# A hybrid layer on Trainium2: u projected by channel and laid out through DRAM, with the forget gates' columns moved into q's first chunk

## The chip, the cores and the metric

The kernel runs on one core of one Trainium2 chip. The metric is the device time of one execution in microseconds (us), the median of several runs. The engines of a core, as the profile names them, are PE (TensorE; PEld is its load of stationary operands), DVE (VectorE), ACT (ScalarE), POOL (GpSimd) and SP (SyncE, which here only issues DMAs).

## What is computed (the reference, cut to what matters)

One layer of a transformer: 1024 tokens of 1024 channels, a mixer of three kinds of heads, then a mixture of 16 experts. All of it is in fp32.

```python
proj = h @ w_in                      # h: 1024 x 1024, w_in: 1024 x 2568
u, q, k, v, f_logit, hc, bg, cg = split(proj, sizes 256, 512, 512, 512, 8, 256, 256, 256)
y_ssm  = s5_mixer(u, ...)            # 16 groups of 16 channels, 64 complex states each: a scan over tokens
y_attn = fox_attention(q, k, v, f_logit + forget_b, ...)   # cum = cumsum(log_sigmoid(f_logit)) biases the logits
y_conv = bg * short_conv(cg * hc)
x = x + gate1 * (rms_norm(concat(y_ssm, y_attn, y_conv)) @ w_out)
...
```

## The kernel before, in words

**Projections.** The normalised input stands transposed in SBUF, channels on the partitions, as two parts hTh and hTl, a rounded high part and the rest. The columns of w_in come in chunks of 256 (hc, cg, bg, u, and two halves each of q, k, v). SP loads each chunk's raw weights in four pieces (`wr`), ACT rounds each piece to its high part `wh` (L262) and POOL forms the low part `wl` (`feed`, L235). A product is then a group of 24 matmuls in `mm3` or `mm3_steps` (L272 to L283): eight of high by high (L275) and eight of low by high (L277), alternating, then eight of high by low (L280), which end the group. With conv's chunks the weights are stationary and 512 tokens move. With q, k and v a 128-token block of hT is stationary and 256 columns of weights move, so there are eight groups for each half of q and 16 for q.

**u.** In the kernel before u is made like q (`uf_group`, L948): eight groups, one for each j in 0 to 7, whose stationary operand is the 128 tokens j, j+8, j+16, ... of hT, a slice with a stride of eight elements, and whose 264 moving columns are u's 256 and the eight of f_logit. ACT writes the group's result into `u_tok` (L953), DVE copies the eight gate columns to `f_sb` (L954). `s5_main` (L769) then turns `u_tok` with 16 PE transposes (L776) and four ACT copies (L777) into `ug`, where a partition is (token within a block of eight, channel of a group) and a column is (group, block of eight).

**The scan.** From `ug` PE makes the blocks' inputs `px` (L790, four sets), DVE multiplies each by powers of the eigenvalue (six operations of `cmul`), runs two scans over 128 blocks (L799, L801), turns the result back (`t`, `vv`), and PE makes the outputs `py` (L826 to L829, four sets), ACT's gelu follows (L831), PE transposes the result for the GLU (L847), multiplies by its weights (`pgl`, L856), and `yd` goes to DRAM (L875).

**The order** is written by hand. Each engine works through its own instructions in the order in which the program issues them. The scan, the conv norm, the forget gates and the second ada product are generators, advanced by `step` (L958) at given places: `side` holds `s5_prep` (which makes the scan's tables; `pg` L684, L686) and then `s5_main`, `side2` holds `conv_norm` (ACT's squares `zt` L913, PE's `pn` L921 and `pb` L938) and later `ada2` (32 loads `adw` of 512 KB on SP, `pr` L1095), `side3` holds `f_chain` (L730). `smalls` (L268) puts a step between two matmuls of a group. US (L62) is the number of matmuls between such steps in u; PY (L57) the number of steps between the scan and `py`. In the loop over q and k (L1115) each group's result `pm` is evicted by ACT (`r`, L1133, and four squares `sq`, L1136); `qk_norm` (L1035) norms four groups at a time (13 small DVE operations `rk_...`, a product on DVE, one on POOL), splits them (`ks`), and `qk_turn` (L1058) transposes them (`ptk` L1061), copies to `qe` (L1067 on DVE, L1069 on ACT) and writes to DRAM from POOL (`qtd`, L1071). In this stage PSUM holds two buffers for `pm`, three for transposes, and three for `px`, `py`, `pgl` and `pr` together.

**f_chain** takes the log of the gates and sums it over tokens. Before, a partition holds a block of eight tokens: a DVE scan inside the block, a matmul with the strict triangle `triS` for the blocks ahead, and `cumd` is written from POOL in elements of 32 bytes for each partition and head.

## Time and profile before

| | |
|---|---|
| median of the runs | 1122.28 us (1121.11, 1122.28, 1126.86) |
| the profiled execution | 1124.22 us, of which the span in the profile is 1122.4 us |
| PE busy | 1026.0 us, 91% of the span |
| DVE, ACT, POOL busy | 722.0, 526.0, 311.7 us |
| stages | conv chunks until 122 us, u to 196, q to 277, k to 373, then v, attention, w_out and the experts |

The profiled execution is 1.94 us above the median, and its time is 1.82 us longer than the span. In the rows below, times are in us from the span's start. A line in the list of instructions gives the start, the duration, the engine, the source line, the operation, what is written and read, the shapes, and how many like it follow at once; in brackets stands the idle time before it and what ended that. A line of a stretch gives its begin, end and length, then the busy time of PE, PEld, DVE, ACT and POOL (with the number of instructions), the granted clock, the DMA engines' mean share and GB/s. A line of loads by form gives the count, the sum and the mean in ns of one. Matmul durations overlap: one matmul starts before the one before it has ended, so what a matmul costs is the distance of the starts. The granted clock (PEclk) is in shares of TensorE's full 2.4 GHz: 0.50 is its lower level, 1.2 GHz.

### The profile page before, as it was taken

The page shows a single profiled execution, that of the slowest core. Times are in us where ns is not written, and L with a number is a line of the kernel's source. Part 1 is how long each engine was busy: PE and PEld are TensorE (multiplying, and loading weights), DVE is VectorE, ACT ScalarE, POOL GpSimd, SP SyncE. Part 2 cuts the span into 40 slices and gives each one's busy share as a digit, 9 for nine tenths or more (in the row PEclk, how much of TensorE's full clock was granted, in tenths as well). Part 3 has the DMA queues.
Part 4 walks back from the last instruction along what each step waited for, and adds up shares of the span by engine and source line. Part 5 has one row for each costly group of instructions (what it writes and reads, how often), then busy time and mean ns, then how long its engine had stood idle before and what let it go on. Part 6 is the DMA issues. An engine that isn't in the chain of part 4 may idle for free. (4 is left out here: it accounts for less than half of the span.)

```text
span 1122.4 us, 18163 instructions
## 1 busy us (share of the span) xinstructions
PE 1026.0 (91%) x6383; PEld 849.1 (76%) x6383; DVE 722.0 (64%) x1564; ACT 526.0 (47%) x1107; POOL 311.7 (28%) x313
## 2 busy tenths in 40 slices
PE   0999899989999999899799994999999999999994
PEld 0578699978887988887688884677777777777773
DVE  2669702583345344687567778796667899789692
ACT  2351111444554555677532321764444676467470
POOL 4215930243321100138222233121422212122130
PEclk9999879989999999899889996799999999999998
DMA  9901103123787343557165733897788799979772
GB/s 190 355 22 39 38 10 78 39 67 110 224 273 255 102 126 105 159 155 230 35 194 188 243 133 107 301 339 244 233 269 281 238 366 357 375 240 353 253 242 41
DMA packets 102366, 213.53 MB, mean 190 GB/s; under 512 B 13998, under 2 KB 37020, under 8 KB 102108
## 3 DMA queue, kind: packets, MB, share of 16 engines
q1 hardware_dynamic: 89744, 170.93, 45.7%
q0 software_dynamic: 11680, 39.55, 13.0%
q10 hardware_dynamic: 828, 1.62, 0.4%
q8 instruction: 62, 1.02, 0.4%
q14 instruction: 52, 0.43, 0.1%
HBM read 184.41 MB, written 27.05 MB: 188 GB/s over the span
## 5 line engine op out<-in xcount | busy, mean ns | idle before, releaser
L94 DVE TENSOR_TENSOR wel<-wer,weh 128x1024 fp32r<-128x1024 f32 x192 | 223.4, 1219 | 2.2 <-ACT weh L1922 1.5
L1922 ACT ACTIVATE weh<-wer 128x1024 fp32r<-128x1024 f32 x192 | 188.9, 1053 | 4.8 <-DVE oh L1931 1.4
L1977 POOL DMA_INDIRECT out_dram<-y,idx x28 | 58.4, 2087 | 227.6 <-DVE y L2042 137.5
L2005 PE MATMUL pg<-weh,xh 128*128 128x512 f32 x256 | 104.7, 409 | 2.0 <-ACT hid L2163 0.7
L2006 PE MATMUL pg<-weh,xl 128*128 128x512 f32 x256 | 103.1, 403 | 0.0
L94 DVE TENSOR_TENSOR pl<-ptp,ph 128x512 fp32r<-128x512 f32 (+1 forms) x80 | 50.3, 636 | 39.5 <-ACT ph L1314 39.2
L2010 PE MATMUL pg<-wel,xh 128*128 128x512 f32 x256 | 66.5, 398 | 0.0
L2005 PEld LDWEIGHTS pg<-weh,xh 128*128 128x128 f32 x256 | 49.1, 192 | 17.9 <-issue 6.1
L1314 ACT ACTIVATE ph<-ptp 128x512 fp32r<-128x512 f32 (+1 forms) x80 | 44.2, 553 | 30.0 <-PE ptp L1309 29.2
L2006 PEld LDWEIGHTS pg<-weh,xl 128*128 128x128 f32 x256 | 49.1, 192 | 11.6 <-DVE xl L94 0.4
L2010 PEld LDWEIGHTS pg<-wel,xh 128*128 128x128 f32 x256 | 47.9, 189 | 11.3
L1296 ACT ACTIVATE lg<-lg,mn 128x128 f32<-128x128 f32 (+3 forms) x64 | 49.5, 774 | 10.6 <-DVE mn L1285 10.5
L1309 PE MATMUL ptp<-identF,lg 128*128 128x128 f32 x288 | 47.9, 285 | 6.2 <-DVE pl L94 6.0
L2032 PE MATMUL pd<-weh,hh 128*128 128x512 f32 x128 | 52.3, 408 | 0.7 <-ACT hh L2024 0.5
L275 PE MATMUL pmw<-woh,yh 128*128 128x512 f32 x128 | 52.7, 411 | 0.0
L277 PE MATMUL pmw<-woh,yl 128*128 128x512 f32 x128 | 51.2, 400 | 0.0
L2033 PE MATMUL pd<-wel,hh 128*128 128x512 f32 x128 | 50.6, 395 | 0.0
L1991 ACT ACTIVATE xh<-ptx 128x512 fp32r<-128x512 f32 x32 | 19.2, 599 | 62.2 <-issue 58.8
L1329 PE MATMUL po<-ph,vs 128*128 128x256 f32 (+1 forms) x160 | 47.1, 316 | 1.2 <-ACT ot L1333 1.0
L1961 POOL DMA_INDIRECT xg<-h2d,idx x16 | 20.7, 1294 | 89.5 <-DVE wgt L1948 62.5
L1330 PE MATMUL po<-pl,vs 128*128 128x256 f32 (+1 forms) x160 | 40.3, 286 | 0.2
L1133 ACT ACTIVATE r<-pm 128x256 f32<-128x256 f32 x32 | 12.3, 384 | 59.7 <-PE pm L280 55.6
(655 smaller groups left out, 2766.2 us busy)
## 6 DMA issues: line engine op xcount, KB each, us to landing
wer<-in_w_up_dram SPq DMA_DIRECT2D x64, 512.0 KB
wer<-in_w_gate_dram SPq DMA_DIRECT2D x63, 512.0 KB
wer<-in_w_down_dram SPq DMA_DIRECT2D x63, 512.0 KB
adw<-in_ada_w_dram SPq DMA_DIRECT2D x32, 512.0 KB
xt<-in_x_dram SPq DMA_DIRECT2D x16, 512.0 KB
vroom<-in_ada_w_dram SPq DMA_DIRECT2D x16, 512.0 KB
qtd<-qe POOLq DMA_DIRECT2D x16, 256.0 KB, 4.1
qt<-qtd SPq DMA_DIRECT2D x16, 256.0 KB
```

Source lines behind the costliest of these rows:

```text
L94: (eng or V).tensor_tensor(o, a, b, op=op)
L275: T.matmul(o, lhsT=sh(k), rhs=mh(k), start=(k == 0), stop=False)
L277: T.matmul(o, lhsT=sl(k), rhs=mh(k), start=False, stop=False)
L1296: A.activation(lg[:, :w], lg[:, :w], AF.Exp, bias=mn, scale=-1.0, accum_out=l_all[:, qb, h:h + 1])
L1309: T.transpose(pt[:, c0:c0 + P], lgs[u, b][0][:, k0:k0 + P], identF)
L1922: A.activation(hi, raw, AF.Copy)
L1977: G.indirect_dma_start(out=out[:, :], out_offset=bass.IndirectOffsetOnAxis(ap=ix, axis=0), in_=y, in_offset=None, compute_op=ALU.add)
L2005: T.matmul(pg, lhsT=x[0][:, k, :], rhs=hi, start=(k == 0), stop=False)
L2006: T.matmul(pg, lhsT=x[1][:, k, :], rhs=hi, start=False, stop=False)
L2010: T.matmul(pg, lhsT=x[0][:, k, :], rhs=lo, start=False, stop=(k == KD - 1))
L2032: T.matmul(pd, lhsT=h[0][:, k, :], rhs=hi[:, n, :], start=(k == 0), stop=False)
L2033: T.matmul(pd, lhsT=h[0][:, k, :], rhs=lo[:, n, :], start=False, stop=False)
```

## The change

u is projected like a conv chunk (`u_group` in place of `uf_group`): the weights of 128 of its channels are stationary and 512 tokens move, four groups of 24 matmuls instead of eight. ACT evicts each group into `uT`, sorted by position within the block of eight. After the second half of each 128 channels, SP writes `uT` to DRAM (`ud`, 512 KB). `s5_main` begins with eight DMAs on POOL's queue, which read `ud` into `ug`, 64 KB each; they stand in POOL's order right behind u's last step. The 16 transposes and four copies are gone. `s5_main` then yields four times (UG), so that `px` comes behind four groups of q; `step` advances it twice per group of q afterwards, so that its later parts run faster; PY is 5. In u, a step comes after every six matmuls instead of 16. The eight gate columns go to q's first half, whose eight groups so have 264 moving columns, and DVE copies them to `f_sb` after each of these groups. `f_chain` now has tokens in order: a scan of the shifted log, then two matmuls (`pcu`) that give the sum for 64 rows of 128 tokens, written in rows of 512 bytes.

```diff
...
 HB = 2
 XA = 1
 XB = 1
-PY = 3
+PY = 5
+UG = 4
 KS = 1
 VN = (2, 2, 12, 2, 2, 2, 10, 2, 2, 2, 2, 2, 10, 2, 2, 2, 2)
 VP = (16, 4, 4)
 FA = 2
-US = 16
+US = 6
 QV = "q"
 PQ = (2, 3, 3)
 BF = dict(cg=(2, 2), bg=(2, 2, 0, 0))
...
     triF = cp.tile([P, P], F32, name="triF")
     G.affine_select(out=triF, in_=onesF, compare_op=ALU.is_ge, fill=0.0, base=0,
                     pattern=[[1, P]], channel_multiplier=-1)
-    triS = cp.tile([P, P], F32, name="triS")
-    tt(triS, triF, identF, ALU.subtract)
     maskF = st.tile([P, P], F32, name="maskF", bufs=1)
     G.memset(maskF, 0.0)
...
     w_in = I["w_in"].rearrange("(k p) n -> p k n", p=P)
-    cols_of = {"u": [(0, 256), (1792, 8)], "hc": [(1800, 256)], "cg": [(2312, 256)], "bg": [(2056, 256)]}
+    cols_of = {"u": [(0, 256)], "hc": [(1800, 256)], "cg": [(2312, 256)], "bg": [(2056, 256)]}
     for nm, base in (("q", 256), ("k", 768), ("v", 1280)):
         for hg in range(2):
             cols_of[nm, hg] = [(base + hg * 256, 256)]
+
+    cols_of["q", 0].append((1792, 8))
     chunks = ["hc", "cg", "bg", "u"] + [(nm, hg) for nm in "qkv" for hg in range(2)]
     parts = ([(ch, k0) for k0 in range(0, KD, 2) for ch in chunks[:2]]
              + [(ch, k0) for ch in chunks[2:] for k0 in range(0, KD, 2)])
...
     yd = dp.tile([S, 256], F32, name="yd")
     cumd = dp.tile([NH, S], F32, name="cumd")
+    ud = dp.tile([256, 8, P], F32, name="ud")
     cd = dp.tile([2, P, S], F32, name="cd")
     es_b = new_stack()
...
     def u_open():
-        X["u_tok"] = room(4096, 16, 128).rearrange("p g (j h) -> p g j h", h=16)
+        X["uT"] = room(4096, 2, 1024).rearrange("p n (j c) -> p n j c", c=P)
         X["f_sb"] = cp.tile([P, NH, 8], F32, name="f_sb")
         X["fb"] = cp.tile([P, NH], F32, name="fb")
         nc.gpsimd.dma_start(out=X["fb"], in_=ap_of(I["forget_b"], 0, [[0, P], [1, NH]]))
...
             yield
         F = [P, NH, 8]
         fs = room(7360, 11, NH * 8).rearrange("p n (h j) -> p n h j", j=8)
-        fl, na, ex, dn, sv, s2, q, lf, d0, cu, nq = (fs[:, n] for n in range(11))
+        fl, na, ex, dn, sv, s2, q, lf, d0, cu, ls = (fs[:, n] for n in range(11))
         tt(fl, X["f_sb"], X["fb"][:, :, None].to_broadcast(F), ALU.add)
         V.scalar_tensor_tensor(na, fl, -1.0, fl, op0=ALU.mult, op1=ALU.min)
         A.activation(ex, na, AF.Exp)
...
         V.scalar_tensor_tensor(lf, q, -2.0, fl, op0=ALU.mult, op1=ALU.add)
         fl_ = lambda x: x.rearrange("p h j -> p (h j)")
-        V.tensor_tensor_scan(fl_(cu), fl_(d0), fl_(lf), 0.0, op0=ALU.mult, op1=ALU.add)
-        tot = cp.tile([P, NH], F32, name="tot")
-        V.tensor_copy(tot, cu[:, :, 7])
-        yield
-        yield
-        po = ps_ms.tile([P, NH], F32, name="pof", tag="ms")
-        T.matmul(po, lhsT=triS, rhs=tot, start=True, stop=True)
-        offs = cp.tile([P, NH], F32, name="offs")
-        V.tensor_copy(offs, po)
-        tt(nq, cu, offs[:, :, None].to_broadcast(F), ALU.add)
-        nc.gpsimd.dma_start(out=cumd[:].rearrange("h (c j) -> c h j", j=8), in_=nq)
+
+        V.memset(ls[:, :, 0:1], 0.0)
+        V.tensor_copy(ls[:, :, 1:], lf[:, :, 0:7])
+        V.tensor_tensor_scan(fl_(cu), fl_(d0), fl_(ls), 0.0, op0=ALU.mult, op1=ALU.add)
+        yield
+        yield
+        pc_ = ps_ms.tile([NH * 8, P], F32, name="pcu", tag="ms")
+        T.matmul(pc_, lhsT=fl_(cu), rhs=onesF, start=True, stop=False)
+        T.matmul(pc_, lhsT=fl_(lf), rhs=triF, start=False, stop=True)
+        nq = room(8064, P)[0:NH * 8, :]
+        V.tensor_copy(nq, pc_)
+        nc.gpsimd.dma_start(out=cumd[:].rearrange("h (i t) -> (h i) t", t=P), in_=nq)
         dump("nq", nq)
         yield
     def s5_main():
-        s5b, wb, kt, tr, ti, car, can, dec, u_tok = (X[n] for n in ("b", "wb", "kt", "tr", "ti", "car", "can", "dec", "u_tok"))
+        s5b, wb, kt, tr, ti, car, can, dec = (X[n] for n in ("b", "wb", "kt", "tr", "ti", "car", "can", "dec"))
         ug = room(0, 16, P)
-        for r4 in range(4):
-            pt = ps_tp.tile([P, 512], F32, name="pt", tag="tp")
-            for q_ in range(4):
-                T.transpose(pt[:, q_ * P:(q_ + 1) * P], u_tok[:, r4 * 4 + q_].rearrange("p i h -> p (i h)"), identF)
-            A.activation(ug[:, r4 * 4:r4 * 4 + 4, :].rearrange("p g c -> p (g c)"), pt, AF.Copy)
-            if r4 == 1:
-                yield
-        yield
+        for i in range(8):
+            nc.gpsimd.dma_start(out=ug[16 * i:16 * i + 16], in_=ud[:, 7 - i, :].rearrange("(g h) c -> h g c", h=16))
+        for _ in range(UG):
+            yield
         t1 = s5b.tile([P, 8, P], F32, name="t1", tag="ta")
         t2 = s5b.tile([P, 8, P], F32, name="t2", tag="tb")
         vv = s5b.tile([P, 2, 8, P], F32, name="vv", tag="wv")
...
             yield
         dump("conv", hcs)
-    hThj = hTh[:].rearrange("p k (c j) -> p k j c", j=8)
-    hTlj = [t[:].rearrange("p (c j) -> p j c", j=8) for t in hTl]
-
-    def uf_group(j):
+    def u_group(cc, hf):
         uh, ul = wt_["u"]
+        cs_, sl = slice(cc * P, cc * P + P), slice(hf * 512, hf * 512 + 512)
         pm = ps_mm.tile([P, 512], F32, name="pm", tag="mm")
-        mm3(pm[:, :264], lambda k: hThj[:, k, j, :], lambda k: hTlj[k][:, j, :],
-            lambda k: uh[:, k, :264], lambda k: ul[:, k, :264])
-        A.activation(X["u_tok"][:, :, 7 - j, :], pm[:, :256].rearrange("p (g h) -> p g h", h=16), AF.Copy)
-        V.tensor_copy(X["f_sb"][:, :, j], pm[:, 256:264])
+        mm3(pm, lambda k: uh[:, k, cs_], lambda k: ul[:, k, cs_],
+            lambda k: hTh[:, k, sl], lambda k: hTl[k][:, sl])
+        A.activation(X["uT"][:, cc, :, hf * 64:hf * 64 + 64], pm[:].rearrange("p (c j) -> p j c", j=8), AF.Copy)
+        if hf:
+            nc.sync.dma_start(out=ud[cc * P:cc * P + P], in_=X["uT"][:, cc])
     side, side2 = [], []
...
     step(20, side2)
     side2.append(conv_norm())
     u_open()
-    for j in range(8):
-        smalls.extend([lambda: None] * US + [step])
-        uf_group(j)
-        if j % 2 == 1:
-            feed(1)
+    for n in range(4):
+        smalls.extend(([lambda: None] * US + [step]) * 3)
+        u_group(n // 2, n % 2)
+        feed(1)
         step(1)
-        step(1, side2)
-    dump("u_tok", X["u_tok"])
+        step(2, side2)
     step(20)
     step(20, side2)
     side3 = [f_chain()]
     side.append(s5_main())
+    step(1)
...
     def project_steps(ch, i, got):
         wh, wl = wt_[ch]
         pm = ps_mm.tile([P, 512], F32, name="pm", tag="mm")
-        yield from mm3_steps(pm[:, :256], lambda k: hTh[:, k, tok(i)], lambda k: hTl[k][:, tok(i)],
-                             lambda k: wh[:, k, :256], lambda k: wl[:, k, :256])
+        m_ = sum(m for _, m in cols_of[ch])
+        yield from mm3_steps(pm[:, :m_], lambda k: hTh[:, k, tok(i)], lambda k: hTl[k][:, tok(i)],
+                             lambda k: wh[:, k, :m_], lambda k: wl[:, k, :m_])
         got.append(pm)
     def project(ch, i):
...
                     pm = project((which, hg), i4 * 4 + i)
                     pmv = pm[:, :256].rearrange("p (h d) -> p h d", d=HD)
                     A.activation(r32[:, i * 4:i * 4 + 4, :], pmv, AF.Copy)
+                    if (which, hg) == ("q", 0):
+                        V.tensor_copy(X["f_sb"][:, :, i4 * 4 + i], pm[:, 256:264])
                     for j in range(4):
                         sq = pk.tile([P, HD], BF16, name="sq", tag="sq")
                         A.activation(sq, pmv[:, j], AF.Square, accum_out=ss[:, i * 4 + j:i * 4 + j + 1])
                     run_later()
                     if i % 2 == 0:
                         feed(1)
-                    step(1)
+                    step(1 if which == "k" or hg * 8 + i4 * 4 + i < UG else 2)
                     step(1 + (which == "k" and i % KS == KS - 1), side2)
                     step(1, side3)
                 qk_norm(which, hg, i4, r32, ss)
```

The order of the instructions, at three places. In them `pm` is a PSUM buffer, `vroom` the SBUF space that `room` hands out (it holds `ug`, `uT`, the scan's tables and results), `wr`, `wh` and `wl` a chunk's raw, high and low weights, `r` and `ks` a normed and a split part of q. On PE, u's groups (before, `pm<-wh,hTh` with hT stationary; the names `wh__1002` and `wh__998` are u's high weights):

```order
L275 MATMUL pm<-wh__1002,hTh 128x264
L277 MATMUL pm<-wh__1002,hTl 128x264
L275 MATMUL pm<-wh__1002,hTh 128x264
L277 MATMUL pm<-wh__1002,hTl 128x264
L280 MATMUL pm<-wl__1003,hTh 128x264 x8
```

and in the changed kernel:

```order
L276 MATMUL pm<-hTh,wh__998 128x512
L278 MATMUL pm<-hTh,wl__999 128x512
L276 MATMUL pm<-hTh,wh__998 128x512
L278 MATMUL pm<-hTh,wl__999 128x512
L281 MATMUL pm<-hTl,wh__998 128x512 x8
```

The groups have become four of 512 columns, and the second matmul of a group already reads a low part of the weights.

On DVE, the two scans in q's stage (`vroom<-vroom,vv`) with what stands around them, before:

```order
L799 SCALAR_TENSOR_TENSOR vroom<-vroom,vv 128x1024
L94 TENSOR_TENSOR ks<-r_1564,ks 128x16x64
L801 SCALAR_TENSOR_TENSOR vroom<-vroom,vv 128x1024
L122 TENSOR_SCALAR rk_m<-ss 128x16
L109 TENSOR_SCALAR rk_i<-rk_m 128x16
```

and in the changed kernel:

```order
L798 SCALAR_TENSOR_TENSOR vroom<-vroom,vv 128x1024
L1133 COPY f_sb<-pm 128x8
L800 SCALAR_TENSOR_TENSOR vroom<-vroom,vv 128x1024
L803 MEMSET vv 128x8
L804 MEMSET vv 128x8
L95 TENSOR_TENSOR t_1613<-tr,vroom 128x1024
L95 TENSOR_TENSOR t_1614<-vroom 128x1024
L1133 COPY f_sb<-pm 128x8
L95 TENSOR_TENSOR ks<-r_1461,ks 128x16x64
L95 TENSOR_TENSOR vv<-t_1613,t_1614 128x8x127
```

The copies of the gate columns out of `pm` now stand between the scan's operations, and the scan's back turn comes ahead of the split `ks`.

On POOL, the end of u's stage and the begin of q's, before:

```order
L728 DMA fb<-in_forget_b_dram 128x8
L94 TENSOR_TENSOR wl__1262<-wr__1011,wh__1261 128x2x256
L94 TENSOR_TENSOR wl__1262<-wr__1050,wh__1261 128x2x256
L94 TENSOR_TENSOR wl__1262<-wr__1054,wh__1261 128x2x256
L94 TENSOR_TENSOR wl__1262<-wr__1265,wh__1261 128x2x256
L94 TENSOR_TENSOR wl__1601<-wr__1362,wh__1600 128x2x256
```

and in the changed kernel:

```order
L730 DMA fb<-in_forget_b_dram 128x8
L95 TENSOR_TENSOR wl__1228<-wr__1006,wh__1227 128x528
L95 TENSOR_TENSOR wl__1228<-wr__1046,wh__1227 128x528
L95 TENSOR_TENSOR wl__1228<-wr__1051,wh__1227 128x528
L95 TENSOR_TENSOR wl__1228<-wr__1231,wh__1227 128x528
L777 DMA vroom<-ud 16x16x128 x8
L95 TENSOR_TENSOR wl__1499<-wr__1298,wh__1498 128x2x256
```

The eight loads stand between the low parts of q's first half and those of its second.

## Rows read from the trace of the kernel before

**Rows 1.** The stretches of q and of k, view of busy times by stretch.

```profile
196.00:277.00 81.00, 75.42 (x599) 70.10 (x600) 47.58 (x100) 36.94 (x173) 27.87 (x21) 0.96 0.21 61
277.00:373.00 96.00, 93.59 (x878) 78.97 (x876) 44.04 (x109) 48.01 (x195) 27.40 (x30) 1.00 0.71 234
```

**Rows 2.** The same view, two stretches of u's stage.

```profile
134.00:143.00 9.00, 8.58 (x36) 6.73 (x36) 0.17 (x1) 3.06 (x6) 8.69 (x11) 0.50 0.23 58
167.00:196.00 29.00, 28.32 (x165) 27.50 (x165) 6.77 (x21) 3.39 (x8) 2.55 (x2) 0.99 0.34 75
```

**Rows 3.** PE's instructions in u, in order of time.

```profile
139.54 0.44 PE L277 MATMUL pm<-wh__1002,hTl 128*128 128x264 f32 x1
142.94 0.44 PE L277 MATMUL pm<-wh__1002,hTl 128*128 128x264 f32 x1
...
167.58 0.40 PE L275 MATMUL pm<-wh__1002,hTh 128*128 128x264 f32 x1
173.38 0.40 PE L275 MATMUL pm<-wh__1002,hTh 128*128 128x264 f32 x1
```

**Rows 4.** PE's instructions in a conv chunk, 24 matmuls apart.

```profile
104.49 0.39 PE L275 MATMUL pm<-hTh,wh__872 128*128 128x512 f32 x1
110.06 0.39 PE L275 MATMUL pm<-hTh,wh__872 128*128 128x512 f32 x1
```

**Rows 5.** Loads of stationary operands, 121 to 300 us, by line and form.

```profile
L277 PEld LDWEIGHTS pm<-wh__1002,hTl 128*128 128x128 f32 x64 | 21.6, 337 | 0.0
L277 PEld LDWEIGHTS pm<-wh__1261,hTl 128*128 128x128 f32 x64 | 12.0, 188 | 0.0
```

**Rows 6.** PE and ACT at the begin of u's stage.

```profile
133.54 0.85 PE L280 MATMUL pm<-wl__1003,hTh 128*128 128x264 f32 x2 [3.44 <-POOL wl__1003 L94]
135.61 0.60 PE L684 MATMUL pg<-car,vroom 64*16 64x128 f32 x2
...
139.78 2.17 ACT L913 ACTIVATE zt<-hcs 128x512 f32<-128x512 f32 x4
```

**Rows 7.** PE in q, groups at two clocks and the idle time.

```profile
237.20 1.11 PE L280 MATMUL pm<-wl__1601,hTh 128*128 128x256 f32 x8
240.06 1.11 PE L280 MATMUL pm<-wl__1601,hTh 128*128 128x256 f32 x8
246.76 0.58 PE L275 MATMUL pm<-wh__1600,hTh 128*128 128x256 f32 x1 [5.58 <-ACT sq L1136]
247.14 0.42 PE L277 MATMUL pm<-wh__1600,hTl 128*128 128x256 f32 x1
250.34 1.91 PE L280 MATMUL pm<-wl__1601,hTh 128*128 128x256 f32 x8
```

**Rows 8.** PE, one of two sets of transposes of `u_tok`.

```profile
198.78 1.03 PE L776 MATMUL pt<-identF,vroom 128*128 128x128 f32 x8
```

**Rows 9.** DVE in q's stage.

```profile
211.52 0.42 DVE L94 TENSOR_TENSOR t<-px,tr 128x256 f32<-128x256 f32 x1 [0.45 <-PE px L790]
213.90 0.17 DVE L122 TENSOR_SCALAR rk_m<-ss 128x16 f32<-128x16 f32 x1
216.41 1.23 DVE L94 TENSOR_TENSOR r<-r,rk_y 128x1024 f32<-128x1024 f32 x1
224.17 2.28 DVE L799 TENSOR_TENSOR_SCAN vroom<-vroom,vv 128x1024 f32<-128x1024 f32 x1
```

**Rows 10.** ACT and POOL in q's stage.

```profile
244.50 0.60 ACT L1069 ACTIVATE qe<-ptk 128x512 f32<-128x512 f32 x1 [8.51 <-DMA qtd<-qe]
240.36 1.11 POOL L1071 DMA_DIRECT2D qtd<-qe  x2
```

**Rows 11.** DMA issues of the page: KB each, us to landing.

```profile
qtd<-qe POOLq DMA_DIRECT2D x16, 256.0 KB, 4.1
```

**Rows 12.** PE in k's stage.

```profile
297.55 1.89 PE L856 MATMUL pgl<-vroom 128*128 128x256 f32 x8
356.77 0.64 PE L1095 MATMUL pr<-adw,cst 128*32 128x256 f32 x8 [2.03 <-DMA adw<-in_ada_w_dram]
```

## The prediction

> **What bounds the kernel now.** I read the stretches first, then PE's instructions inside them, then what PE waits for. In the stretches of q and k PE is busy 75.42 of 81.00 us and 93.59 of 96.00 us, and no other engine comes near it [rows 1]; near the end of u it is busy 28.32 of 29.00 us [rows 2]. So PE's order is the clock of these stages: what leaves PE leaves the time, unless another engine then comes last. The profiled execution (1124.22 us) is the one that all durations come from; it lies 1.94 us above the median, which I take off at the end.
>
> u is slow per column. Its 264-column matmuls start 5.80/24 = 0.242 us apart at a granted clock of 0.99 [rows 2, 3], and at a clock of 0.50 also 3.40/14 = 0.243 us apart [rows 2, 3]. A pitch that does not change with the clock is not set by the columns. Conv's matmuls, of 512 columns, take 5.57/24 = 0.232 us [rows 4], and q's groups of 256 columns 2.86 us, or 0.12 us a matmul [rows 7]. What differs in u is the stationary operand, tokens eight apart: its loads take 337 ns, those of q's first half, of adjacent tokens, 188 ns [rows 5]. Thus u pays for 512 columns a matmul and uses half.
>
> **u.** Both kernels meet the same wait for POOL's low parts, 3.44 us, and are through with it at 135.61 us [rows 6]. In the new order the low parts are needed earlier in a group, so PE waits at an earlier matmul, but for the same last piece. From there the old kernel has seven groups, 168 x 0.242 = 40.6 us. The new one by its order has about 81 of its 96 matmuls left, 81 x 0.232 = 18.8 us: **-21.8 us**. Conv's matmuls have the very form of the new ones, so I trust that price.
>
> After that wait the clock is at its lower level [rows 2]. There q's 256 columns take 3.20/15 = 0.213 us [rows 7], so 512 would take 0.427 us, 0.195 us more. After the wait at 246.76 us the low clock held through one group, some 5 us of dense matmuls [rows 7]; I take 7 of u's, **+1.4** (0 to 15.8, if all 81 run so). ACT's four squares for the conv norm, 2.17 us [rows 6], now stand behind an eviction that comes sooner relative to them; about half may show, **+1.0** (0 to 2.2). u's sum is **-19.4 us**.
>
> The Trainium skill, TensorE: Matmul & The Clock Gate, section Back-to-back issue gap, gives an isolated matmul N/2.4 + 2.5 ns, and the section LDWEIGHTS lets a load depend on its columns alone. By these u's old groups would cost 168 x 112 ns = 18.8 us (an estimate from that page), its new ones 81 x 216 ns = 17.5 us, and the change would bring 1.3 us there. Rows 3 and 5 show 0.242 us and two load times for one shape, so the measurement decides.
>
> **The way through DRAM.** The new path takes the place of two sets of eight transposes, 1.03 us each with the overlap, some 0.8 without [rows 8]: **-1.6 us**. In return `px` must wait until the last load has landed. After u's last group: an eviction (0.6, as one of 512 columns in [rows 10]), the SP write of 512 KB, eight issues on POOL, the last landing. 256 KB from POOL land in 4.1 us [rows 11]; I take that for each of the two transfers, though one is twice and one a quarter of that size. Two issues take 1.11 us [rows 10], so eight 4.4. Together 13.2 us, plus some hand-over. In that time PE has the conv norm's 16 small matmuls and four groups, 4 x 2.9 = 11.6. I take a wait of **+2** (0 to 6, the upper end if the write takes twice as long). Behind the eight issues on POOL stand the low parts of q's second half; PE needs them four groups later, so they cost nothing unless that wait grows past 10 us. The SP writes stand between raw loads of later chunks; those are far ahead. The Trainium skill, DMA: Bandwidth & Descriptors, section on the SWDGE path, gives about 2.0 us plus bytes/436e3: by it 256 KB would take 2.6 us, where the row has 4.1, and the path would be done in time, which takes those 2 us out of the sum.
>
> **q.** The eight gate columns add 8 x 24 x 8 columns at 2.4 GHz = **+0.6**. They bring a new wait: the copy to `f_sb` must be done before a `pm` buffer, of which there are two, is free, and DVE's order puts these copies between the scan's operations. From `px` on DVE has, up to the eighth copy: four sets of six products at 2.38 [rows 9], the norm at 2.51 + 1.23 [rows 9], two scans at 2.28 [rows 9], two products of the back turn, as wide as the norm's, at 1.23, and the copies: 9.5 + 3.7 + 4.6 + 2.5 + 1 = 21.3 us, and 22 with its start. The ninth copy's group waits behind this. PE in that time has five groups and the four sets of `px`, each put at a set of transposes: 14.3 + 3.2 = 17.5. So **+5** in small pieces (0, if DVE keeps ahead, to 9, with another norm in between). `py` needs 6 us more of DVE, which two groups and the transposes cover.
>
> The old kernel lost 5.58 us at 246.76, when ACT waited 8.51 for the transfer of `qe` that POOL had issued late, and its next group ran at half clock, 2.26 us longer [rows 7, 10], with a slower set of transposes: 8.2 us. In the new order this chain (norm, POOL's product, issue at 1.11 for two, landing 4.1) comes as late after `px`, but PE then has sets of `py` and a group to do. I take **-8.2** off and put back **+1.5** (0 to 8.2, the whole loss). q's sum is -1.6 + 2 + 0.6 + 5 - 8.2 + 1.5 = **-0.7 us**. Two further steps a group move the GLU's transposes and `pgl` from k to q; on PE they cost the same in either.
>
> **k.** That move takes three sets like the 1.89 of [rows 12], and the transposes, some 7.5 us, out of k, so its 32 loads of 512 KB have less time. The stage already moves 234 GB/s with DMA engines 0.71 busy [rows 1], and one wait for such a load of 2.03 us stands at its end [rows 12]. I take **+2** (0 to 7.5). The gates' sum and `cumd` are used only by attention, far later: 0.
>
> **Sum:** -19.4 - 0.7 + 2 = -18.1 us, 1106.1 for a profiled execution, 1104.2 for the median. I forecast **1104 us**, and 1098 to 1111 for this case alone.
>
> **Rivals.** A measurement of this kernel can tell about 0.5%, 5.6 us, from no change.
>
> A. *As forecast*, 0.70.
>
> B. *No new waits in q*: loads in time, DVE ahead of PE. For it speak the small idle shares of q now. The 8.5 us of the three waits go: 1096. 0.10.
>
> C. *k is bound by its loads*: the 7.5 us moved out come back in full, 5.5 more: 1110. For it the 2.03 us, against it a DMA share of 0.71. 0.07.
>
> D. *The round trip is late* by 8 more, as 512-byte runs in eight transfers might be, with a part at low clock: 1112.5. 0.06.
>
> E. *The slow pitch belongs to 264 columns, not to the stride.* Then q's first half becomes slow: 8 x 24 x (0.242 - 0.122) = +23, of which the three waits, 8.5, hide under it: 1119, no change by the bound. Against it stand the load times and the pitch that ignores the clock [rows 3, 5]. 0.04. The Trainium skill's rule on loads (TensorE: Matmul & The Clock Gate, section LDWEIGHTS) stands on this rival's side.
>
> F. *Slower.* One wait for `px` takes the clock down, as the waits of 3.44 and 5.58 us did [rows 2, 6, 7], and the small waits for `f_sb` keep it there. Each group at the low clock costs 5.12 - 2.86 = 2.26 more, and hides 6.5 us of waits. It undoes the gain at (18.1 + 6.5)/2.26 = 10.9 groups, and goes past 0.5% at 13.3. Through q's last 12 and four of k: 36.2 - 6.5 = +29.7, 1134. Against it: after 246.76 the clock was back within a group or two, and k's stage holds 1.00 with a wait of 2.03 us in it [rows 1, 12]. 0.03.
>
> A, B, C and D are faster by over 0.5%: 0.93; E is 0.04, F 0.03. The range 1094 to 1114 holds A to D.
>
> **What would show it.** Right: u's 512-column matmuls 0.232 us apart and its last group done near 175 us, not 195; no idle time of 5 us near the fourteenth group of q; waits of about 2 us for `f_sb` in groups 7 to 10 of q; q's 264 columns 0.12 us apart. Wrong: PEclk of 0.5 through u's 512-column groups; a long idle time ahead of the first `px`, released by a DMA; `adw` ending PE's waits all through k; a gap before attention that was not there.

## The result and the profile after

The changed kernel takes 1114.12 us (median of six, 1113.35 to 1115.96), the kernel before in the same comparison 1122.32 us: a ratio of 0.9927, 95% interval 0.991 to 0.9944. The forecast was 1104 us, so 18 us were expected and 8.2 came. The profiled execution of the changed kernel has a span of 1114.2 us, against 1122.4.

The first matmul of each chunk in PE's list cuts both spans into the same stages (us):

| | u | q | k | from v to the end | span |
|---|---|---|---|---|---|
| before | 73.5 | 80.8 | 80.7 | 765.1 | 1122.4 |
| changed | 53.0 | 92.5 | 80.9 | 765.5 | 1114.2 |
| difference | -20.5 | +11.7 | +0.2 | +0.4 | -8.2 |
| forecast | -19.4 | +6.8 | -5.5 | 0 | -18.1 |

(The forecast for q and k has here the 7.5 us of the GLU that move from one to the other.) u gave about what was expected (in a second profile of the changed kernel, e18 below, u is 55.8 us and its gain 17.7); q and k took some 5 and 6 us more than expected.

The table of the kernel before lets k end at 373 us. The first matmul on v's weights stands at 357.34, so the second line of [rows 1] holds 15.7 us of v. Its two parts, k and the begin of v:

```profile
276.64:357.34 80.70, 78.29 (x738) 65.05 (x736) 36.87 (x91) 42.40 (x184) 22.62 (x26) 1.00 0.79 263
357.34:373.00 15.66, 15.66 (x148) 14.29 (x144) 7.53 (x19) 5.98 (x12) 5.14 (x5) 1.00 0.26 83
```

In k alone the DMA engines were 0.79 busy and not 0.71.

PE's list in u and q of the changed kernel, where [rows 3, 4] stood before:

```profile
160.57 0.39 PE L276 MATMUL pm<-hTh,wh__998 128*128 128x512 f32 x1
163.36 0.39 PE L276 MATMUL pm<-hTh,wh__998 128*128 128x512 f32 x1
...
175.57 0.29 PE L278 MATMUL pm<-wh__1227,hTl 128*128 128x264 f32 x1
175.69 0.28 PE L276 MATMUL pm<-wh__1227,hTh 128*128 128x264 f32 x1
```

The first two are 12 matmuls apart: 2.79/12 = 0.232 us, conv's price. The last two show the 264 columns with adjacent tokens as stationary operand, 0.12 us apart.

All idle time of PE of more than 0.8 us in q and k, with what it was put down to, by which the waits of [rows 7, 12] are to be read:

```profile
182.30 0.39 PE L276 MATMUL pm<-wh__1227,hTh 128*128 128x264 f32 x1 [0.85 <-ACT sq L1136]
190.95 1.41 PE L789 MATMUL px<-vroom 128*64 128x128 f32 x16 [2.54 <-DMA vroom<-ud]
192.29 0.59 PE L276 MATMUL pm<-wh__1227,hTh 128*128 128x264 f32 x1
196.62 1.97 PE L789 MATMUL px<-vroom 128*64 128x128 f32 x32
...
208.66 0.59 PE L276 MATMUL pm<-wh__1227,hTh 128*128 128x264 f32 x1 [2.81 <-ACT sq L1136]
213.29 0.39 PE L276 MATMUL pm<-wh__1498,hTh 128*128 128x256 f32 x1
218.88 0.58 PE L276 MATMUL pm<-wh__1498,hTh 128*128 128x256 f32 x1 [2.48 <-ACT sq L1136]
223.35 0.80 PE L1059 MATMUL ptk<-identR,ks 128*128 128x128 f32 x8
...
287.07 1.05 PE L1093 MATMUL pr<-adw,cst 128*32 128x256 f32 x8 [2.01 <-DMA adw<-in_ada_w_dram]
319.81 0.64 PE L1093 MATMUL pr<-adw,cst 128*32 128x256 f32 x8 [3.26 <-DMA adw<-in_ada_w_dram]
```

Three waits in q's first ten groups, of 2.54, 2.81 and 2.48 us, stand where there was one of 5.58. After each of them a group takes long: 196.62 - 192.29 = 4.33 us, 213.29 - 208.66 = 4.63 and 223.35 - 218.88 = 4.47, against 3.03 for the first group of q (175.34 to 178.37 in the same list) or 2.86 for a group of 256 columns [rows 7]. The busy times by stretch say why (begin, end, length, then PE, PEld, DVE, ACT, POOL, the granted clock, DMA share, GB/s):

```profile
175.30:267.80 92.50, 83.14 (x619) 76.48 (x617) 41.62 (x90) 36.25 (x170) 27.61 (x28) 0.94 0.32 82
267.80:348.70 80.90, 75.26 (x702) 62.88 (x700) 42.36 (x109) 40.29 (x179) 23.70 (x26) 0.96 0.74 250
133.00:138.00 5.00, 4.57 (x20) 3.16 (x21) 0.65 (x1) 0.00 (x0) 4.84 (x7) 0.60 0.45 108
138.00:145.00 7.00, 7.00 (x46) 4.74 (x44) 0.00 (x0) 2.57 (x5) 6.76 (x7) 1.00 0.00 0
190.00:196.00 6.00, 5.05 (x36) 4.75 (x37) 2.36 (x6) 0.00 (x1) 0.00 (x0) 0.72 0.23 68
196.00:202.00 6.00, 6.00 (x68) 5.55 (x68) 4.41 (x17) 2.08 (x11) 0.91 (x1) 1.00 0.00 1
208.00:214.00 6.00, 5.34 (x30) 5.20 (x31) 5.90 (x8) 2.57 (x17) 0.16 (x1) 0.72 0.02 4
```

After a wait of 2.5 to 2.8 us the clock is at its lower level for part of a group and back in the next; in u, after POOL's 3.39 us, too (third and fourth line). k is 80.9 us long with PE busy 75.26; before, it was as long with PE busy 78.29.

What the squares that end two of the waits had waited for, in ACT's list:

```profile
201.75 0.38 ACT L1131 ACTIVATE r<-pm 128x256 f32<-128x256 f32 x1 [2.95 <-PE pm L281]
207.68 0.22 ACT L1136 ACTIVATE sq<-pm 128x64 bf16<-128x64 f32 x1 [5.55 <-DVE f_sb L1133]
...
217.91 0.22 ACT L1136 ACTIVATE sq<-pm 128x64 bf16<-128x64 f32 x1 [3.87 <-DVE f_sb L1133]
```

The row put PE's wait down to ACT, and ACT had stood 5.55 us for DVE's copy of the gate columns from the same `pm`. In DVE's list those copies come at the end of the products and of the back turn:

```profile
207.49 0.17 DVE L1133 COPY f_sb<-pm 128x8 f32<-128x8 f32 x1
217.71 0.16 DVE L1133 COPY f_sb<-pm 128x8 f32<-128x8 f32 x1
```

The way through DRAM in POOL's list and in the list of DMA issues between 150 and 195 us:

```profile
178.94 4.49 POOL L777 DMA_DIRECT2D vroom<-ud  x8 [2.87 <-PE pm L281]
```

```profile
ud<-vroom SPq DMA_DIRECT2D x2, 512.0 KB, 4.1
...
vroom<-ud POOLq DMA_DIRECT2D x8, 128.0 KB, 5.7
```

A write lands in 4.1 us, the eight issues take 4.49, the landing 5.7. Each of the eight reads is of 128 KB; the 64 KB that the text on the change gives for them is wrong.

### The profile page after: what moved, and what is told of

Read it like the earlier page. It is cut to its first block, busy times and chain, and to the rows that moved or that the text cites. A ratio compares the mean times of both kernels' runs of the same rounds, so it can differ in the third digit from the quotient of the medians.

```text
span 1114.2 us, 17973 instructions
## 1 busy us (share of the span) xinstructions
PE 1009.2 (91%) x6273; PEld 825.0 (74%) x6273; DVE 719.1 (65%) x1563; ACT 523.4 (47%) x1099; POOL 315.4 (28%) x321
## 5 line engine op out<-in xcount | busy, mean ns | idle before, releaser
L1977 POOL DMA_INDIRECT out_dram<-y,idx x28 | 62.3, 2227 | 226.8 <-DVE y L2042 137.7
```

Of the source, the lines that this page charges most:

```text
L1977: G.indirect_dma_start(out=out[:, :], out_offset=bass.IndirectOffsetOnAxis(ap=ix, axis=0), in_=y, in_offset=None, compute_op=ALU.add)
```

## The experiments

The jobs ran on several chips, and the changed kernel run again on one of them (e18, at the end) gave 0.9951, interval 0.9923 to 0.9979. So a ratio is worth no more than some three tenths of a per cent, and the stages of the profiles carry more than the ratios. But each profile is of one execution: the executions of one kernel lie up to 10 us apart (e1: 1108.79 to 1119.23), u is 53.0 to 56.1 us long in runs that do not touch it, and from v to the end it takes 761.9 us in e2, 765.2 in e18 and 769.8 in e7, with the same work. All edits but e11's are made to the changed kernel. Ratio and interval are to the kernel before on the same chip; stages as above.

| | us | ratio | interval | u | q | k |
|---|---|---|---|---|---|---|
| e1 gates on ACT | 1114.93 | 0.9929 | 0.9900-0.9958 | 55.7 | 88.9 | 84.9 |
| e2 UG 6 | 1116.87 | 0.9956 | 0.9933-0.9979 | 55.6 | 92.0 | 82.8 |
| e3 GLU in k | 1116.63 | 0.9963 | 0.9946-0.9981 | 56.0 | 88.6 | 82.9 |
| e4 half of adw | 1186.53 | 1.0605 | 1.0557-1.0652 | 55.7 | 91.6 | 74.8 |
| e5 gates in q's 2nd half | 1125.83 | 1.0023 | 0.9998-1.0048 | 56.0 | 97.9 | 79.0 |
| e6 AY 0 | 1119.19 | 0.9972 | 0.9944-1.0000 | 55.7 | 88.1 | 89.0 |
| e7 UG 6, PY 7 | 1112.55 | 0.9908 | 0.9879-0.9938 | 55.7 | 84.8 | 80.7 |
| e8 e5 + e6 + e7 | 1110.69 | 0.9888 | 0.9835-0.9942 | 56.1 | 84.7 | 82.3 |
| e9 qe's writes off POOL | 1118.63 | 0.9962 | 0.9939-0.9985 | 53.0 | 92.6 | 85.8 |
| e10 e7 + e9 | 1120.86 | 0.9971 | 0.9949-0.9993 | 55.7 | 90.8 | 88.6 |
| e11 before, no stride | 1188.59 | | one run | 55.5 | 79.8 | 84.3 |
| e12 less DVE | 1105.46 | | one run | 53.2 | 86.1 | 78.7 |
| e13 finer adw | 1118.20 | 0.9947 | 0.9919-0.9975 | 55.6 | 94.6 | 82.5 |
| e14 e7 + e13 | 1111.13 | 0.9904 | 0.9874-0.9934 | 53.1 | 84.9 | 82.2 |
| e15 e1 + e13, UG 5 | 1117.52 | 0.9955 | 0.9930-0.9980 | 55.9 | 91.6 | 81.1 |
| e16 back turn later | 1117.89 | 0.9966 | 0.9939-0.9992 | 53.1 | 94.4 | 80.7 |
| e17 e16 + e13 | 1118.26 | 0.9958 | 0.9941-0.9976 | 56.0 | 94.2 | 80.9 |
| e18 changed, again | 1118.00 | 0.9951 | 0.9923-0.9979 | 55.8 | 92.3 | 81.6 |

q's length alone misleads, since the order of the steps also decides how much of the GLU's work stands in q and how much in k. Of its 32 matmuls `pgl`, 24 stand in q in the changed kernel and in most runs, 8 in e15, and none in e2, e3, e7, e8, e10, e14, e16 and e17. What can be compared is the sum of q and k: 161.5 us before, 173.4 in the changed kernel, 173.9 in e18.

**Is u's price the stride?** e11, on the kernel before:

```diff
-    hThj = hTh[:].rearrange("p k (c j) -> p k j c", j=8)
-    hTlj = [t[:].rearrange("p (c j) -> p j c", j=8) for t in hTl]
+    hThj = hTh[:].rearrange("p k (j c) -> p k j c", j=8)
+    hTlj = [t[:].rearrange("p (j c) -> p j c", j=8) for t in hTl]
```

> The kernel before with one edit: u's stationary operands are 128 adjacent tokens of hT instead of tokens eight apart, so u's values come in another order of tokens and the scan runs over a wrong order; the instructions are the same. If the slow pitch of 0.242 us comes from the stride, it falls to about 0.122 us, the loads from 337 to 188 ns, and u from 73 to 51 us, as short as with the four groups of 512 columns; if it belongs to u's 264 columns or to other work beside it, 0.242 us stays.

Groups of 24 end 162.72 - 159.79 = 2.93 us apart, 0.122 us a matmul, and u takes 55.5 us, against 53.0 and 55.8 in the two profiles of the changed kernel, with the clock at 0.50 right after POOL's wait and 1.00 at the end:

```profile
159.79 1.13 PE L280 MATMUL pm<-wl__1003,hTh 128*128 128x264 f32 x8
162.72 1.13 PE L280 MATMUL pm<-wl__1003,hTh 128*128 128x264 f32 x8
```

```profile
L277 PEld LDWEIGHTS pm<-wh__1002,hTl 128*128 128x128 f32 x64 | 14.2, 223 | 0.0
```

The loads fall from 337 [rows 5] to a mean of 223 ns, part of them at the low clock. So the whole gain in u belongs to the stride; eight groups of 264 adjacent tokens are as good as four of 512. (The time of this run, 1188.59, is later work on other values; its stages up to v are comparable.)

**The copies of the gates.** e1, and e5, which moves the columns to the second half:

```diff
-                        V.tensor_copy(X["f_sb"][:, :, i4 * 4 + i], pm[:, 256:264])
+                        A.activation(X["f_sb"][:, :, i4 * 4 + i], pm[:, 256:264], AF.Copy)
```

> The changed kernel with one edit: the copy of the eight gate columns to f_sb runs on ACT instead of DVE. Theory 1 (the two waits of 2.81 and 2.48 us ahead of q's eighth and tenth group, and the low clock after each, some 1.6 us a time, come from the copies that stand in DVE's order behind the scan): both waits go, q becomes 8 us shorter, about 1106 us. Theory 2 (the chain from DVE's norm over POOL and the transfer of qe holds q's later groups anyway): the waits go, but PE then stops as long at a group after the first py, and the time stays at 1114 us.

Both waits went, q fell by 3.6 us only, and the time not at all. In q a wait for DVE's split `ks` took their place:

```profile
219.55 0.63 PE L1059 MATMUL ptk<-identR,ks 128*128 128x128 f32 x5 [2.79 <-DVE ks L95]
```

and k grew by 4.0. Neither theory as written: the first was right on the waits, the second on what followed, though the new wait is DVE's and not POOL's.

```diff
-    cols_of["q", 0].append((1792, 8))
+    cols_of["q", 1].append((1792, 8))
...
-                    if (which, hg) == ("q", 0):
+                    if (which, hg) == ("q", 1):
```

> The changed kernel with the gates' eight columns in q's second half instead of the first, their copies still on DVE. Theory 1 (the copies behind the scan on DVE cost q two waits and two low clocks, and what that gives is then eaten by k's loads, as with the copies on ACT): the waits of 2.81 and 2.48 us in q's first ten groups go, q falls from 92 to about 87 us, and k grows, so the time falls by less than 3 us, 1111 to 1114. Theory 2 (q's shortening counts in full): 1108 us.

A miss: q became longer, 97.9. The waits of 2.81 and 2.48 went; one of 2.49 for `ks` and one of 4.94 in the second half came, and one of 2.68 for the GLU's weights; the second of them:

```profile
225.58 0.59 PE L276 MATMUL pm<-wh__1496,hTh 128*128 128x264 f32 x1 [4.94 <-ACT sq L1136]
```

**Where px stands.** e2, and e7 with PY = 7 as well:

```diff
-PY = 5
-UG = 4
+PY = 7
+UG = 6
```

> The changed kernel with UG = 6 instead of 4: px and the scan come two groups of q later. Theory 1 (the round trip through DRAM lands 2.5 us late for four groups, and the wait takes the clock down for a group): the wait of 2.54 us for ud and about 1.5 us of low clock go, 1110 us, if the waits for f_sb only move along with the scan. Theory 2 (with the scan later, more f_sb copies come ahead of it, so fewer groups wait behind DVE): down to 1105 us. Theory 3 (DVE's chain behind the scan sets the end of q): each group later costs, 1114 to 1117 us.

The waits for `ud` and `f_sb` went, all three; `py` waited for DVE's back turn instead, 5.85 and 2.85 us, and q stayed at 92.0, although the 24 `pgl` had left it. The third theory fits.

```profile
227.19 0.79 PE L826 MATMUL py<-car,vv 64*128 64x128 f32 x2 [5.85 <-DVE vv L95]
230.84 0.79 PE L828 MATMUL py<-can,vv 64*128 64x128 f32 x2 [2.85 <-DVE vv L95]
```

> The changed kernel with UG = 6 and PY = 7: px and the scan two groups of q later, and py two steps behind that. Theory 1 (with UG = 6 alone the waits for ud and f_sb went, but py came ahead of DVE's back turn and waited 5.85 and 2.85 us): those waits go too, q is near 84 us with part of the GLU in k; k stays load-bound at 81 to 83 us, so about 1108 us. Theory 2 (the time at which k's loads begin sets the end of k, and it moves only as q's length does): q's whole gain shows, 1106 us. Theory 3: a new wait ahead of py or gt, 1114 us.

q fell to 84.8 and k held 80.7, with 2.12 us of waits for `adw` left in it. The sum of the two is 165.5, 7.9 less than in the changed kernel. But PE waits in q as long as there: a single wait of 9.40 us came, at the same place in the chain as the old one of [rows 7]. What left q is the GLU's work (its 24 `pgl` and 8 of its 16 transposes), and k took it in without growing:

```profile
231.67 0.58 PE L276 MATMUL pm<-wh__1498,hTh 128*128 128x256 f32 x1 [9.40 <-ACT sq L1136]
```

From v to the end it took 769.8 us, 4.3 more; e14, with the same order in q, took 762.3, so no run shows that the edit did this. The time, 1112.55, has the ratio 0.9908 on its chip. The first theory had the lengths of q and k, and the third the new wait.

**The chain of qe.** e9 on the changed kernel and e10 on e7's:

```diff
-            nc.gpsimd.dma_start(out=qtd[i4 * 4 + n, hg], in_=o_)
+            (nc.sync if n % 2 else nc.scalar).dma_start(out=qtd[i4 * 4 + n, hg], in_=o_)
```

> The changed kernel with the writes of qe to DRAM issued by ACT (its own copies) and by SP (DVE's copies) instead of by POOL, where they stand behind POOL's product of r and a low part of weights. Theory 1 (one chain, DVE's norm, POOL's product, the issue, the landing of qe, can stop q; in the changed kernel PE has lost its time already to px and f_sb and has py to do meanwhile, so the chain costs nothing there): ACT's wait of 8.97 us for qe goes, the waits for px and f_sb stay, and the time falls by less than 3 us, 1111 to 1114. Theory 2 (ACT's wait delays gelu and the GLU and so the end of q): 1107 us.

q did not change, 92.6 against 92.5, with the waits of 2.83 and 2.48 us in their places: in the changed kernel POOL's chain costs q nothing, as the first theory had it. k grew to 85.8, since SP now had these writes between its loads of `adw`.

> The same edit on the kernel of e7 (UG = 6, PY = 7), where PE waited 9.40 us at 231.67 for a group's squares that stood behind ACT's copy to qe. Theory 1: that wait and the low clock after it, some 2 us, go, q falls from 85 to 74 us, and the time from 1112.5 to about 1102; k's loads begin earlier with it. Theory 2 (another wait, DVE's ks or py, takes its place): 1109 to 1112 us.

The wait is the second theory's: PE waited 9.11 us where it had waited 9.40, now for `ks`.

```profile
233.85 0.37 PE L1059 MATMUL ptk<-identR,ks 128*128 128x128 f32 x1 [9.11 <-DVE ks L95]
```

The time, 1120.86, is above both theories, and q is 90.8 us, 6.0 longer than in e7, with the same work on PE and no more waiting. The first two lines are q in e10 and 15 us behind the wait, the other two the same of e7:

```profile
176.86:267.61 90.75, 80.72 (x587) 73.85 (x585) 43.02 (x88) 31.18 (x159) 26.41 (x20) 0.85 0.33 84
235.00:250.00 15.00, 15.00 (x50) 11.42 (x49) 2.83 (x8) 4.11 (x15) 3.56 (x2) 0.50 0.19 61
177.16:261.96 84.80, 74.39 (x586) 69.16 (x585) 43.71 (x88) 31.01 (x159) 30.14 (x28) 0.94 0.36 90
237.00:252.00 15.00, 15.00 (x102) 12.58 (x101) 2.78 (x5) 6.38 (x24) 5.30 (x6) 0.99 0.19 57
```

In e7 a whole group of q stood behind the wait, and the clock was back when `py`'s sets came. In e10 they came right behind it, after eight transposes, and those up to 250 us ran at 0.50. The same order stands behind the waits for DVE's back turn in e2 and e16, with 0.50 from 231 to 246 and from 239 to 254 us and 0.87 and 0.86 as the mean of q. So q of e10 pays some 6 us more to the clock than q of e7, for waits of the same length. k grew to 88.6, with SP's writes between its loads as in e9.

**DVE's queue.** e12 takes work off DVE alone; e16 changes its order, and puts all copies to `qe` and their writes on ACT:

```diff
-            cmul(vr[:, sl], vi[:, sl], px[:, 0], px[:, 1], tr[:, sl], ti[:, sl], t1[:, sl], t2[:, sl])
+            tt(vr[:, sl], px[:, 0], tr[:, sl], ALU.mult)
+            tt(vi[:, sl], px[:, 1], ti[:, sl], ALU.mult)
```

> The changed kernel with two instead of six DVE operations for each of the four px sets: the sums and the cross products of the complex multiplication are left out, some 1.6 us of DVE a set, 6.3 in all; PE's work is the same. Theory 1 (in q PE waits for DVE's one queue, from px over the scans and the back turn to the split ks, whichever of the copies, ks or qe the wait is then put down to): the waits of 2.81 and 2.48 us fall by most of 5 us with their low clocks, q from 92 to about 86 us. Theory 2 (POOL, the transfers or ACT hold q): q stays at 92.

q went from 92.5 to 86.1 us, while PE's work was the same and DVE's busy time in q fell from 41.63 to 34.55. Of the two waits one of 1.92 us was left:

```profile
214.48 0.38 PE L276 MATMUL pm<-wh__1498,hTh 128*128 128x256 f32 x1 [1.92 <-ACT sq L1137]
```

PE's waits in q fell by 3.0 us in sum, and its busy time by 3.4 (79.69 against 83.11), for with the waits the low clock behind them went (granted clock 0.98 against 0.94). So DVE's queue from `px` to `ks` makes these waits. That the 6.4 us of q meet the 6.3 taken off is partly chance, and the run is a single one on other values.

```diff
-PY = 5
-UG = 4
+PY = 2
+UG = 6
...
-QV = "q"
+QV = ""
...
+        for _ in range(5):
+            yield
         V.memset(vr[:, :, 0:1], 0.0)
         V.memset(vi[:, :, 0:1], 0.0)
...
-            nc.gpsimd.dma_start(out=qtd[i4 * 4 + n, hg], in_=o_)
+            nc.scalar.dma_start(out=qtd[i4 * 4 + n, hg], in_=o_)
```

> UG = 6; the scan's back turn five steps later and PY = 2, so that DVE reaches the split ks of q's second four groups ahead of it; and all copies to qe and their writes on ACT, so that neither DVE nor POOL has them. Theory 1 (PE's wait of 9 us in e7 and e10 is DVE's queue: the back turn ahead of ks): the wait goes, py is covered by q's last groups, q about 77 to 80 us with most of the GLU in k, k 81 to 85: 1104 to 1108. Theory 2 (py comes too late at q's end, or ACT's wait for qe's landing holds the evictions): a wait of 5 us or more ahead of py or of a group, 1112.

The wait for `ks` shrank to 0.59 us, and `py` waited for the back turn, 3.44 and 8.71 us; q was 94.4. That is the second theory. DVE had less to do than in e2 (busy 40.17 us in q against 43.80), and q was longer all the same: the order chooses who waits, and what stands behind the wait on PE sets what the clock adds.

```profile
224.38 0.88 PE L1061 MATMUL ptk<-identR,ks 128*128 128x128 f32 x8 [0.59 <-DVE ks L95]
228.99 0.60 PE L828 MATMUL py<-car,vv 64*128 64x128 f32 x2 [3.44 <-DVE vv L95]
238.30 0.79 PE L830 MATMUL py<-can,vv 64*128 64x128 f32 x2 [8.71 <-DVE vv L95]
```

**k.** e3 leaves most of the GLU in k, e4 halves the loads:

```diff
-                    step(1 if which == "k" or hg * 8 + i4 * 4 + i < UG else 2)
+                    step(1 if which == "k" or hg * 8 + i4 * 4 + i < UG or hg else 2)
```

> The changed kernel with one step instead of two in the last eight groups of q, so that most of py's later sets come at q's end and the GLU's transposes and pgl fall into k again. Theory 1 (k is bound by its 32 loads of adw and has the same 81 us with the GLU in it or without): q about 7 us shorter, k the same 81, about 1107 us. Theory 2 (PE bounds both): what leaves q comes back in k, 1114 us.

q fell by 3.9 us and not 7, since its waits stayed (2.82, 2.48 and one more of 2.06); k with the GLU in it was 82.9, only 2 us longer than without, so the sum fell to 171.4. The waits for `adw` became 3.7 us in place of 5.6.

```diff
-            if n < 32:
+            if n < 32 and n % 2:
+                ws.append(ws[-1])
+            elif n < 32:
```

> The changed kernel with 16 instead of 32 loads of adw: every second block of the second modulation's weights is left out, its matmuls read the block before it again, so PE does the same work on half the bytes and the modulation's values are others. Theory 1 (k is bound by these loads): the three waits for adw, 5.6 us, and the low clock after them, some 2 us, go; k falls from 81 to 73 us, about 1106.5 us. Theory 2 (something else holds k at 81 us): waits for another transfer or engine take their place, 1114 us.

k fell by 6.1 us, to 74.8, and no wait for `adw` was left. The stretch of k in this run, to set against the second line of the changed kernel's above:

```profile
267.05:341.82 74.77, 72.85 (x702) 61.47 (x700) 43.31 (x109) 40.53 (x179) 24.43 (x26) 0.98 0.53 172
```

The same 702 instructions of PE take 74.8 us in place of 80.9. (The run's total, 1186.53, comes from behind k, where the layer works on other values.) So the loads hold k in the changed kernel. With the GLU in it PE holds k as well: busy 78.29 of 80.70 us before, 78.22 of 80.70 in e7 and 80.90 of 82.17 in e14, at a clock of 1.00.

Whether it is the buffers' grain, e13:

```diff
-AD2 = 3
+AD2 = 6
...
-            if n < 32:
-                w = pk2.tile([P, 1024], F32, name="adw2", tag="adw2", bufs=AD2)
-                nc.sync.dma_start(out=w, in_=adaw[:, n % 8, 2048 + n // 8 * 1024:3072 + n // 8 * 1024])
+            if n < 64:
+                w = pk2.tile([P, 512], F32, name="adw2", tag="adw2", bufs=AD2)
+                c0 = 2048 + n // 16 * 1024 + n % 2 * 512
+                nc.sync.dma_start(out=w, in_=adaw[:, n // 2 % 8, c0:c0 + 512])
```

> The changed kernel with the second modulation's weights in 64 loads of 256 KB and six buffers instead of 32 of 512 KB and three: the same bytes and the same space. Theory 1 (k is held by three buffers, each of which comes free only after all of its 512 KB has been used): the loads run more evenly, the waits for adw fall from 5.6 to some 2 us, k from 81 to about 77, the time by 3 to 4 us. Theory 2 (the rate of the loads holds k): no change, or slower by the issues on SP.

k was 82.5, with 5.0 us of waits for `adw`, one of them 4.31. The grain alone does not shorten k. Whether the bytes in flight (three times 512 KB in either) or the rate of the transfers holds k stays open; no run here tells them apart.

```profile
322.74 0.64 PE L1094 MATMUL pr<-adw,cst 128*32 128x256 f32 x2 [4.31 <-DMA adw<-in_ada_w_dram]
```

An earlier begin, e6:

```diff
-AY = 3
+AY = 0
```

> The changed kernel with AY = 0 instead of 3: the second modulation's first product comes one group into k instead of three steps later, so its buffers come free and its loads run on from there, in a stretch where the DMA engines are now 0.41 busy. Theory 1 (k is set by when its 32 loads can run, three buffers at a time): k falls by about 4 us, from 81 to 77, 1110 us. Theory 2 (the loads are bound by the rate of the DMA engines or by what else moves): the waits for adw stay as long in sum, 1114 us.

A miss: k became 89.0, while v and what follows became 5.8 shorter. The turn of `ks` waited 7.62 us for DVE, which had stood 8.24 us for a transfer of `qe`:

```profile
311.24 1.25 PE L1059 MATMUL ptk<-identR,ks 128*128 128x128 f32 x8 [7.62 <-DVE ks L95]
```

```profile
309.01 0.69 DVE L1065 COPY qe<-ptk 128x512 f32<-128x512 f32 x1 [8.24 <-DMA qtd<-qe]
```

**Together.** e8 is e5, e6 and e7; e14 is e7 and e13; e15 is e1 and e13 with `UG = 5`; e17 is e16 and e13.

> The changed kernel with the edits of e5, e6 and e7 together: gates in q's second half, UG = 6, PY = 7, AY = 0. If q's waits and k's loads are what the change lost, both go: q near 83 us, k near 77, about 1102 us. If the rest is of another kind, not below 1108.

> UG = 6 and PY = 7 (e7) with the finer loads of e13. If both theories of e7 and e13 hold, k no longer takes back what q gives: 1108 us or less, against 1112.5 for e7 alone.

> The gate copies on ACT (e1), UG = 5 and the finer loads of e13: the waits for ud and f_sb go; what DVE's queue still holds shows at ks. q near 86 us, k near 77: about 1105 us. If k's loads are bound by rate, 1112.

> The kernel of e16 with the finer loads of e13. Theory 1: as e16, and 1 to 3 us less where the loads hold k: 1102 to 1106. Theory 2 (the loads' rate holds k): as e16.

> The changed kernel as it is, on the same chip as e16 and e17, to set them against: 0.993 of the kernel before, as measured at first.

e8 and e14 (and e7) have the lowest ratios, 0.9888 to 0.9908. e8, at 1110.69, was not the 1102 us of its first case (q 84.7 and k 82.3 for 83 and 77), and e14, at 1111.13, not 1108 or less: its waits for `adw` were down to 1.0 us, and with the GLU in it k still took 82.2. The wait of 8 to 10 us in q is still there (9.51 in e14, 8.34 in e8):

```profile
226.32 0.75 PE L1059 MATMUL ptk<-identR,ks 128*128 128x128 f32 x4 [8.34 <-ACT qe L1067]
```

e15 got rid of the waits for `ud` and `f_sb` and had 6.25 us ahead of `py`, with q at 91.6 and k at 81.1 instead of 86 and 77; e17 was as e16. No version is clear of the changed kernel's own first ratio of 0.9927; against e18's 0.9951, on another chip, the intervals of e7 and e14 overlap as well. That any of them beats it is likely by the stages (q and k 165.5 to 167.1 in sum against 173.4 and 173.9) and not shown by the times.

## Why the prediction was wrong

It had the sign and the parts right, and two terms of the sum too small. By its own steps:

- **u, -19.4 forecast, -20.5 found.** The pitch of 0.232 us, the same wait for POOL (3.39 us after, 3.44 before) and a few matmuls at the low clock came as worked out; the wait for ACT's squares was 0.76 us where 1.0 stood. That it comes so near is partly luck: in e18's profile the low clock lasts longer, and the gain is 17.7. That the stride sets the price is shown by e11. Its rival E is out: 264 columns with adjacent tokens run 0.122 us apart.
- **The way through DRAM, +2 forecast, 2.54 found**, from a landing of 4.1 us for the write, 4.49 for the issues and 5.7 for the loads.
- **The gates' copies, +5 forecast, 2.81 + 2.48 found.** These waits were right to a few tenths of a us. That they come from DVE's queue is shown by e12, and that taking any one of them away brings another from the same queue, by e1, e2, e10 and e16.
- **The chain of `qe`, +1.5 forecast, nothing found.** The 0.68 us that PE waits for ACT's copy to `qe` ahead of a transpose for the GLU stays (0.69) when e9 takes the writes off POOL.
- **q, the step that failed first.** The text gave each wait its idle time and nothing for the clock, because the wait of 2.03 us at the end of k had left the clock of that stage at 1.00 [rows 1, 12]. The waits of q took it down: 4.33, 4.63 and 4.47 us for groups of 3.03, 3.03 and 2.86 are 4.5 us in all. Rival F had the mechanism, and for this kernel a wrong end: the clock was back after each group, so it cost 4.5 us and not 36 (e10 shows the dearer end, some 6 us more). The gate columns cost 0.17 us a group (3.03 against 2.86), 1.4 and not 0.6, and one more wait of 0.85 us was not foreseen. The GLU's part that moved from k to q was 6.3 us and not 7.5 (24 `pgl` at 4.9, twelve transposes at 1.4). 4.5 + 0.8 + 0.9 - 1.2 are 5.0, and the waits above nearly cancel (+0.5, +0.3, -0.8); q was 4.9 us longer than forecast.
- **k, the step that failed most: +2 forecast, 7.7 found** (7.5 moved out, 0.2 longer; with the 6.3 us that really moved, 6.5). The text weighed the loads and took a value near the lower end, since the DMA engines were 0.71 busy on the mean. That mean has 15.7 us of v in it; k alone had 0.79. Rival C was the case: what left PE came back as waits for `adw` (5.3 us against 2.0) and as low clock behind them, and with half the loads (e4) k is 6.1 us shorter. Nor does the mean alone tell: it is 0.74 in the changed kernel, where the loads do hold k. What left k left a stage whose end was set by something else as well.

The two together are some 10 us, which is the whole difference. The range ended at 1114 and the median came out at 1114.12: C alone, or the clock alone, was inside it, both together were not, and the text had treated them as alternatives.

## What to carry to other kernels

A stage in which one engine is busy throughout can be held by a second one to nearly the same length (here 80.7 and 80.9 us): before counting what leaves it as gain, ask what else ends there, and work out the stage without the first. Work that moves between two stages is compared by the sum of the two. When several waits on one in-order queue look like separate terms, price the queue: in e1, e2, e10 and e16 another order passed the wait on, and in e12 less work shortened the stage. And an idle time of TensorE like those of q (2.5 to 2.8 us) is to be counted with the low clock behind it: here 1.3 to 1.6 us where a full group of matmuls followed, and some 6 us in e10, where a long row of small ones did.

## What was not expected of the hardware

- ACT's squares of a group waited 5.55 us for DVE's copy of eight other columns of the same `pm`. The order in the program, copy ahead of squares, made a slow reader on one engine hold a reader on another; no run here puts the copy behind them.
- The wait of 2.03 us at the end of k before showed no low clock behind it (1.00 in the begin of v), nor did one of 1.92 us in e12 (1.00 from 214 to 220 us). 2.01 us in k after was followed by a stretch (287 to 292 us) at a granted clock of 0.66; in q waits of 2.48 to 2.81 us were each followed by six us at 0.72. What decides was not tried.
- The changed kernel's u takes 53.0 to 53.2 us in some profiles and 55.6 to 56.1 in others. The wait for POOL's low parts in it was 3.4 to 4.1 us in the former and 4.0 to 5.1 in the latter, with the clock right after it (133 to 138 us) at 0.60 in the changed kernel's first profile and 0.50 in e1's and e18's.
- Two of DVE's operations in q took longer than others of their shape: 2.09 us where 0.43 is usual, and 2.13 where 1.22 is. They add 2.6 us to the queue that the gates' copies stand in, which was 25.2 us long from `px` to the last copy (192.46 to 217.71) and not 22. POOL was at work beside both; that this is the cause is not shown, since no run moves POOL's work alone.

```profile
201.66 2.09 DVE L95 TENSOR_TENSOR vv<-t,t 128x256 f32<-128x256 f32 x1
214.52 2.13 DVE L95 TENSOR_TENSOR t<-tr,vroom 128x1024 f32<-128x1024 f32 x1
...
201.09 2.37 POOL L95 TENSOR_TENSOR r<-r,gq 128x1024 f32<-128x1024 f32 x1 [12.13 <-DVE r L95]
213.84 1.73 POOL L95 TENSOR_TENSOR wl__1499<-wr__1502,wh__1498 128x512 fp32r<-128x512 f32 x1 [8.93 <-ACT wh__1498 L263]
```
